# One set of four PSUM banks for units and down products, turned router products and a first gather of one expert pair in a two-layer decoder with a mixture of experts

## The chip, the cores and the metric

One core of a Trainium2 chip runs the whole program. The metric is device time in microseconds; a time is the median of several executions. TensorE (PE) multiplies matrices and writes into PSUM, which is divided here into eight banks of 512 float32 per partition; VectorE (DVE) and ScalarE (ACT) read the banks and write SBUF; GpSimd (POOL) computes a little and starts the indirect loads; the sync engine (SP) starts the loads of weights. Each engine works off its own instructions in program order and waits on semaphores for the others.

## What is computed

Two layers on 512 tokens of 1024 elements. Each layer has a mixer (attention and gated linear attention behind one projection) and then a mixture of 32 experts, four groups of eight: the router picks one group per token and two experts in it. The change lies in the second half.

```python
grp_prob = softmax(hf @ w_router_grp + b_router_grp)
grp_w, grp_idx = top_k(grp_prob, 1)
exp_logits = (hf @ w_router_exp + b_router_exp).reshape(-1, N_GROUPS, EXPERTS_PER_GROUP)
sel_logits = take_along_axis(exp_logits, grp_idx[:, :, None], axis=1)[:, 0]
top_logit, top_idx = top_k(sel_logits, 2)
top_w = softmax(top_logit) * grp_w
...
for g in range(N_GROUPS):
    a = einsum('nd,edf->nef', hf, w_gate[g])
    u = einsum('nd,edf->nef', hf, w_up[g])
    y = y + einsum('nef,efd->nd', silu(a) * u * comb[:, g, :, None], w_down[g])
```

Here `hf` is the normalised and modulated token, `comb` holds each token's weight for each expert (nought but for two), and `x = x + gate_f * y` ends the layer.

## The kernel before

Tokens stand in four tiles of 128 (`tt`), the 1024 elements in eight blocks of 128 (`k`). The kernel computes each expert on its own tokens only: 64 slots per expert, two experts (a pair) side by side in 128 rows, 16 pairs per layer. What would not fit in 64 slots goes through a loop at the end, which runs no iteration with these inputs.

**Router products.** `logits` (L860) runs while the mixer's output gets ready, for the first four `k`; `logits_of` (L874) does the last four `k` of one token tile. Both transpose `x` on PE into a bank of the tag `att` (three banks), copy it to SBUF (`xT`, by DVE and ACT in turns) and multiply it with the 36 columns of `wr`: tokens come out on the partitions, 36 logits each, all in one `misc` bank named `lg`. After that ACT writes the normalised tokens (`xn`, four operations at L923), and the POOL queue stores them to DRAM as `xg` (issued by the helper at L88). DVE makes `lo` out of `lg` (L937), one operation for each token tile.

**Selection** (L940 to L998, and L1207 on). DVE finds the group (`first_max`, L941), the two experts (`eid`, `ex`) and, with counting products on PE (`rk`), the slot of every token (`pos`, `slot`). `ohp` is a table of ones at the slots; `by_slot` (L1213) multiplies it with token numbers (`exn`) and gives a list of which token stands in which slot (`nv`), and `numbered` (L994) turns that into row numbers `idx`. `keep_warm` (L80) puts products whose result nobody reads into PE's queue. `fetch` (L1000) gathers 128 rows of `xg` by `idx`. The softmax weights of group and experts (`gs`, `gw`, `den`, `cw`) stand in the program behind the fetches.

**Expert loop.** `gather` (L1007) transposes fetched rows on PE into two banks of the tag `g` and evicts them with scale and shift to `gT`. Before the change it takes the rows of two pairs at a time, 256 columns, two `k` in a bank. `hidden` (L1035) makes the gate and up products (`gu`, one bank) and `hs`; `turn` (L1053) transposes `hs` and copies it to `hT`; `down` (L1062) makes two banks `d` of products and DVE scales them to `o`, which ACT and POOL split into `ohi` and `olo`; `places` (L1102) makes the table `oT` that brings slots back to tokens; `combine` (L1112) does one of eight units (a token tile and half of the columns): two products `y` into a bank, and DVE's `add` (L1092) onto `x`. `weights_by_slot` (L1248) comes once, behind the first pair's gate and up products.

In the program PE's order is: down products of pair i − 1, gate and up products of pair i, then the eight units of pair i − 1 with the transposes of rows for later pairs between them, and behind the sixth unit the transposes of `hs`:

```python
for u in range(4):
    for v in range(2):
        if i:
            combine(2 * u + v, *part)
    next(rest, None)
    if u == 2:
        hT = turn(hs)
```

PSUM in this half: `y` two banks (units, `keep_warm`, `slots`), `d` two, `g` two, `gu` one, `misc` one. A bank is taken again when everything that read it is done. `pm` and `tc.keep_in_program_order` pin the order of what they wrap; the rest may be moved by the scheduler between their dependences. The last two pairs are combined together by `combine_last` (L1120), whose units use banks of all tags.

SP's queue starts the weights: gate and up of an expert into one of five buffers `wgu`, down into one of four `wd`, four loads behind every `hidden`.

## Time and profile before

| | us |
|---|---|
| median of three runs | 1285.71 (1284.75 to 1287.04) |
| profiled execution, whole | 1283.96 |
| profiled execution, span of its instructions | 1282.1 |
| PE busy | 1172.3 (91%) |
| DVE busy | 797.0 (62%) |
| ACT busy | 462.7 (36%) |
| POOL busy | 307.0 (24%) |
| DMA, mean over the span | 244 GB/s |

The granted PE clock was 0.969 of full speed in the mean. A row of the page's groups reads: line, engine, operation, what is written and what is read, count; then busy time and mean ns of one; then the engine's idle time just ahead of these instructions and who ended most of it. PEld is PE's loading of stationary operands, which runs beside the products. A row of the order of time has the start, the busy time, and in brackets the idle time before it and its releaser. A product of float32 shows as two records in the trace. The lines that the argument rests on stand in the prediction.

### The profile page before, as it was taken

The numbers are of one execution on the slowest core, as the hardware profiler recorded it, in microseconds if no ns is written. First come the engines' busy times: TensorE is split into PE (matmuls) and PEld (weight loads), VectorE is DVE, ScalarE is ACT, GpSimd is POOL, SyncE is SP. The second block draws the span as 40 slices with busy tenths as digits, with TensorE's granted clock in tenths as the row PEclk, the third lists the DMA queues.
The fourth block names the chain that finished last, engine by engine and source line by source line (L and its number), as shares of the span: only waits on it lengthen the run. The fifth ranks groups of instructions, "written<-read, shape, count | busy, mean of one in ns | idle before, by whom it ended". The sixth has DMA issues, their size and how long they took to land. (4 is left out here: it accounts for less than half of the span.)

```text
span 1282.1 us, 16510 instructions
## 1 busy us (share of the span) xinstructions
PE 1172.3 (91%) x5935; PEld 739.7 (58%) x5935; DVE 797.0 (62%) x1484; ACT 462.7 (36%) x922; POOL 307.0 (24%) x330
## 2 busy tenths in 40 slices
PE   4989978977998999999988999899998899999996
PEld 2677746655885444444447877667787444444443
DVE  3488969796544555555546988877655355555553
ACT  3366635553251111111124775554535111111111
POOL 2122232244212222221103212434421222112110
PEclk9989989998979999999998999999998999999999
DMA  8454675751485999999805547763158699999961
GB/s 282 149 178 129 205 188 161 233 160 55 186 342 174 390 394 392 392 392 376 325 1 175 161 127 227 169 172 129 50 217 325 219 385 399 399 392 386 387 253 67
DMA packets 106285, 312.28 MB, mean 244 GB/s; under 512 B 13176, under 2 KB 50284, under 8 KB 81624
## 3 DMA queue, kind: packets, MB, share of 16 engines
q1 hardware_dynamic: 96920, 289.62, 62.6%
q0 software_dynamic: 9280, 21.57, 4.9%
q8 instruction: 48, 0.79, 0.3%
q14 instruction: 37, 0.30, 0.1%
HBM read 311.10 MB, written 8.43 MB: 249 GB/s over the span
## 5 line engine op out<-in xcount | busy, mean ns | idle before, releaser
L74 PE MATMUL proj<-whl,hh 128*128 128x512 f32 (+2 forms) x768 | 220.6, 370 | 7.4 <-ACT whl L95 6.2
L78 PE MATMUL gu<-wgu,gT 128*64 128x512 f32 x1024 | 225.8, 593 | 0.0
L1095 DVE TENSOR_TENSOR x<-y,x 128x512 f32<-128x512 f32 x240 | 153.9, 684 | 14.1 <-PE y L78 14.1
L78 PEld LDWEIGHTS gu<-wgu,gT 128*64 128x64 f32 x1024 | 73.5, 137 | 146.1 <-issue 146.1
L74 PEld LDWEIGHTS proj<-whl,hh 128*128 128x128 f32 x768 | 135.5, 191 | 36.1 <-issue 7.7
L1088 POOL TENSOR_TENSOR olo<-o,ohi 128x512 fp32r<-128x512 f32 x60 | 76.4, 1274 | 301.8 <-ACT ohi L1087 301.8
L96 POOL TENSOR_TENSOR whl<-raw,whl 128x512 fp32r<-128x512 f32 (+2 forms) x80 | 90.0, 1128 | 238.3 <-ACT whl L95 184.4
L1050 DVE TENSOR_TENSOR hs<-hs,gu 128x256 f32<-128x256 f32 x32 | 13.5, 421 | 204.4 <-ACT hs L1049 204.4
L74 PE MATMUL proj<-whl,hl 128*128 128x512 f32 (+2 forms) x384 | 139.0, 363 | 0.1
L255 DVE SCALAR_TENSOR_TENSOR row<-wada,ct,row 128x512 f32<-128x512 f32 x140 | 119.9, 856 | 16.8 <-DMA wada<-in_w_ada_dram 15.6
L78 PE MATMUL y<-ohi,oT 128*128 128x512 f32 x240 | 116.1, 484 | 6.9 <-DVE x L1095 6.9
L78 PE MATMUL d<-wd,hT 128*64 128x512 f32 x512 | 116.9, 598 | 1.4 <-ACT hT L1059 1.4
L1028 ACT ACTIVATE gT<-g,mod 128x256 f32<-128x256 f32 x64 | 35.9, 565 | 177.3 <-DVE gT L1030 177.3
L78 PE MATMUL y<-olo,oT 128*128 128x512 f32 x240 | 94.6, 394 | 0.0
L95 ACT ACTIVATE whl<-raw 128x512 fp32r<-128x512 f32 (+2 forms) x128 | 66.2, 524 | 68.3 <-PE proj L74 36.6
L78 PEld LDWEIGHTS y<-ohi,oT 128*128 128x128 f32 x240 | 44.8, 186 | 74.8 <-DVE x L1095 45.4
L74 PEld LDWEIGHTS proj<-whl,hl 128*128 128x128 f32 x384 | 72.6, 189 | 13.4 <-issue 3.0
L1049 ACT ACTIVATE hs<-gu 128x256 f32<-128x256 f32 x32 | 12.3, 384 | 169.9 <-PE gu L78 169.9
L78 PEld LDWEIGHTS d<-wd,hT 128*64 128x64 f32 x512 | 33.9, 136 | 62.2 <-issue 59.9
L1082 DVE SCALAR_TENSOR_TENSOR o<-d,cws,gate_f 128x512 f32<-128x512 f32 x64 | 47.7, 748 | 34.9 <-PE d L78 34.9
L1087 ACT ACTIVATE ohi<-o 128x512 fp32r<-128x512 f32 x60 | 37.8, 629 | 78.9 <-DVE o L1082 78.8
L1003 POOL DMA_INDIRECT rows<-xg,idx x32 | 32.8, 1025 | 126.0 <-PE g L1022 108.9
(339 smaller groups left out, 2041.6 us busy)
## 6 DMA issues: line engine op xcount, KB each, us to landing
wgu<-in_w_gate_dram SPq DMA_DIRECT2D x64, 1024.0 KB, 7.7
wgu<-in_w_up_dram SPq DMA_DIRECT2D x64, 1024.0 KB, 10.3
wd<-in_w_down_dram SPq DMA_DIRECT2D x64, 1024.0 KB, 8.8
wada<-in_w_ada_dram SPq DMA_DIRECT2D x96, 512.0 KB, 4.3
raw<-in_w_in_dram SPq DMA_DIRECT2D x80, 256.0 KB, 3.6
raw<-in_w_out_dram SPq DMA_DIRECT2D x16, 512.0 KB, 3.7
raw<-in_w_in_dram SPq DMA_DIRECT2D x32, 128.0 KB, 2.9
xg<-xn POOLq DMA_DIRECT2D x8, 512.0 KB, 2.9
```

The lines of the kernel that those rows point to most:

```text
L74: T.matmul(o, a, b, start=start, stop=stop, skip_group_check=True)
L78: tc.keep_in_program_order(T.matmul(o, a, b, start=start, stop=stop, skip_group_check=True))
L95: A.activation(hi, src, AF.Copy)
L96: eng.tensor_tensor(lo, src, hi.bitcast(F), op=OP.subtract)
L255: V.scalar_tensor_tensor(row, ws[k], ct1[:, k:k + 1], row, op0=OP.mult, op1=OP.add)
L1003: G.indirect_dma_start(r, None, xg[:, :], bass.IndirectOffsetOnAxis(ap=idx, axis=0), bounds_check=S - 1, oob_is_err=False)
L1028: A.activation(o, src, AF.Identity, scale=m, bias=b)
L1050: V.tensor_tensor(hs[r], hs[r], gu[r, 256:512], op=OP.mult)
L1082: V.scalar_tensor_tensor(o, pd, cws[:, i:i + 1], gate, op0=OP.mult, op1=OP.mult)
L1087: A.activation(hi, o, AF.Copy)
L1088: (G if last is None else V).tensor_tensor(lo, o, hi.bitcast(F), op=OP.subtract)
L1095: V.tensor_tensor(xc, ps, xc, op=OP.add)
```

## The change

It has five parts.

1. `logits` and `logits_of`: `wr` is now the stationary operand and `xT` the moving one, so that 36 logits come out on the partitions and tokens along the row. Even `k` add up on partitions 0 to 35, odd `k` on 64 to 99 of the same bank (`lgT`). For each token tile GpSimd clears a tile, DVE copies the one part and ACT the other into it, and one product with the constant `two_parts` adds both and turns them round into `lg`, which now takes one of the three `att` banks. `lo` is made in two operations over all tiles.
2. The list: token numbers start at 1 − 65536, so that `numbered` is one operation for the whole list; `ohp` is one table of 64 columns per entry, and `by_slot` makes two products of 64 by 16 where one of 128 by 32 was; the last `keep_warm` has 20 products, not 14.
3. The softmax weights are issued behind the list.
4. The first gather takes the rows of the first pair alone (128 columns, four `k` in a bank); the second pair's is put behind the first pair's gate and up products.
5. `y`, `d`, `warm` and `slots` share one tag `dy` of four banks.

The diff, cut to its core:

```diff
@@ keep_warm, down, combine, add_rows, weights_by_slot
-        ps = bank("warm", "y", 2)
+        ps = bank("warm", "dy", 4)
...
-                pd = bank("d", "d", 2)
+                pd = bank("d", "dy", 4)
...
-            ps = bank("y", "y", 2)
+            ps = bank("y", "dy", 4)
...
-                ps = bank("slots", "y", 2)
+                ps = bank("slots", "dy", 4)
@@ constants
+    two_parts = const.tile([P, 36], F, name="two_parts")
+    V.tensor_tensor(two_parts, ident[:, 0:36], ident[:, 64:100], op=OP.add)
...
-    G.iota(tok_i, pattern=[[P, NT]], base=1, channel_multiplier=1)
+    G.iota(tok_i, pattern=[[P, NT]], base=1 - 65536, channel_multiplier=1)
@@ logits
-            for tt in range(NT):
-                mm(lg[:, tt], t[:, P * tt:P * tt + P], wr[:, k], tt == 0 and k == 0, k == KT - 1)
+            o = 64 * (k % 2)
+            mm(lg[0][o:o + 36], wr[:, k], t, k < 2, False)
@@ logits_of
+        c = slice(P * tt, P * tt + P)
         for k in range(4, KT):
-            mm(lg[:, tt], t[:, P * (k - 4):P * (k - 3)], wr[:, k], False, k == KT - 1)
+            o = 64 * (k % 2)
+            mm(lg[0][o:o + 36, c], wr[:, k], t[:, P * (k - 4):P * (k - 3)], False, k >= KT - 2)
+        t = s2([P, P], name="lgT")
+        G.memset(t, 0.0)
+        if lg[1] is None:
+            lg[1] = att("lg")[:, 0:NT * 36].rearrange("p (t e) -> p t e", t=NT)
+        for i, copy in enumerate((V.tensor_copy, A.copy)):
+            r = slice(64 * i, 64 * i + 36)
+            copy(t[r], lg[0][r, c])
+        mm(lg[1][:, tt], t, two_parts, tt == 0, True)
@@ moe
-        for tt in range(NT):
-            V.scalar_tensor_tensor(lo[:, tt], lg[:, tt], rs[:, tt:tt + 1], lc, op0=OP.mult, op1=OP.add)
+        V.tensor_tensor(lo, lg, rs[:, :, None].to_broadcast([P, NT, 36]), op=OP.mult)
+        V.tensor_tensor(lo, lo, lc[:, None, :].to_broadcast([P, NT, 36]), op=OP.add)
@@ numbered
-            none = tiny.tile(list(idx.shape), F, name="none")
-            V.tensor_scalar(none, ps, 0.0, 65536.0, op0=OP.is_equal, op1=OP.mult)
-            V.scalar_tensor_tensor(idx, ps, -1.0, none, op0=OP.add, op1=OP.add)
+            return V.tensor_scalar(idx, ps, 65535.0, None, op0=OP.add)
@@ gather
-                for k2 in range(KT // 2):
+                nk = 512 // n
+                for k0 in range(0, KT, nk):
...
-                    for k in (2 * k2, 2 * k2 + 1):
+                    for k in range(k0, k0 + nk):
@@ by_slot and the list
-            lst = misc(name, [P, NE])
+            lst = misc(name, [P, NE // 2])
             for i in range(NT * 2):
-                pm(lst, ohp[i // NT][:, i % NT].rearrange("p a s -> p (a s)"), values[:, i], i == 0, i == NT * 2 - 1)
+                for a in range(2):
+                    pm(lst[64 * a:64 * a + 64], ohp[:, i], values[:, i, a::2], i == 0, i == NT * 2 - 1)
...
-        nv = by_slot(exn, "nv")
-        for a in range(2):
-            numbered(nv[64 * a:64 * a + 64, :, a], idx[64 * a:64 * a + 64])
-        keep_warm(lo.rearrange("p t e -> p (t e)"), 14)
+        listed = numbered(by_slot(exn, "nv"), idx)
+        keep_warm(lo.rearrange("p t e -> p (t e)"), 20)
...
+        with tc.issue_after(listed.ins):
...
@@ first pairs
-        gT, rest = gather(fetched[0:2])
+        gT, rest = gather(fetched[0:1])
         for _ in rest:
             pass
+        gT1, second = gather(fetched[1:2])
...
             if i == 0:
+                for _ in second:
+                    pass
                 weights_by_slot()
```

What is left out: the first two pairs read their tokens from column 0 of `gT` and `gT1`, `combine_last` and the loop for overflow name `dy` where they named `y` and `d`, and the lines of the softmax weights are indented under `issue_after`.

Three places show how instructions move. In these rows, each is one engine's instruction with its output, its inputs and its size, an `x` with a count where it repeats, and in brackets the engines or DMA queues whose semaphores it waits for. The first is PE's queue at the end of one burst in the middle of layer 0's loop: `y` are the units' products, `g` transposed rows, `d` the down products. Before:

```order
L78 MATMUL y<-ohi,oT 128x512 [waits DVE_49]
L78 MATMUL y<-olo,oT 128x512
L78 MATMUL y<-ohi,oT 128x512 [waits DVE_49]
L78 MATMUL y<-olo,oT 128x512
L1022 MATMUL g<-ident,rows 128x128 x2
L78 MATMUL d<-wd,hT 64x512 [waits DMAHW0_49,Activation_49]
L78 MATMUL d<-wd,hT 64x512 [waits DMAHW1_49]
L78 MATMUL d<-wd,hT 64x512 x2
L78 MATMUL d<-wd,hT 64x512 [waits PE_49]
L78 MATMUL d<-wd,hT 64x512 x3
```

After:

```order
L78 MATMUL y<-ohi,oT 128x512 [waits DVE_49]
L78 MATMUL y<-olo,oT 128x512
L78 MATMUL y<-ohi,oT 128x512 [waits DVE_49]
L78 MATMUL y<-olo,oT 128x512
L1035 MATMUL g<-ident,rows 128x128 x2
L78 MATMUL d<-wd,hT 64x512 [waits DMAHW0_49,DVE_49,Activation_49]
L78 MATMUL d<-wd,hT 64x512 [waits DMAHW1_49]
L78 MATMUL d<-wd,hT 64x512 x2
L78 MATMUL d<-wd,hT 64x512 [waits DVE_49]
L78 MATMUL d<-wd,hT 64x512 x3
```

The order is the same; the first `d` and the fifth now wait for DVE as well, where the fifth waited for PE before.

The second is PE's queue at the end of layer 0's router products: `xT` are the transposes of `x`, `lg` and `lgT` the products with `wr`, `warm` the products of `keep_warm`. Before:

```order
L74 MATMUL lg<-wr,xT 128x36 [waits DVE_49]
L74 MATMUL lg<-wr,xT 128x36 x3
L879 MATMUL xT<-ident,x 128x128 x3
L74 MATMUL lg<-wr,xT 128x36 [waits Activation_49]
L74 MATMUL lg<-wr,xT 128x36 x3
L879 MATMUL xT<-ident,x 128x128 [waits PE_49]
L879 MATMUL xT<-ident,x 128x128 x3
L74 MATMUL lg<-wr,xT 128x36 [waits DVE_49]
L74 MATMUL lg<-wr,xT 128x36 x3
L74 MATMUL lg<-wr,xT 128x36 [waits Activation_49]
L74 MATMUL lg<-wr,xT 128x36 x3
L78 MATMUL warm<-lo,ident 128x144 [waits DVE_49]
```

After (the lines of the code have moved by four):

```order
L883 MATMUL xT<-ident,x 128x128 [waits PE_49]
L883 MATMUL xT<-ident,x 128x128 x3
L74 MATMUL lgT<-xT,wr 36x128 [waits Activation_49]
L74 MATMUL lgT<-xT,wr 36x128 x3
L883 MATMUL xT<-ident,x 128x128 [waits PE_49]
L883 MATMUL xT<-ident,x 128x128 x3
L74 MATMUL lg<-two_parts,lgT 128x36 [waits Activation_49]
L74 MATMUL lgT<-xT,wr 36x128 x4
L74 MATMUL lg<-two_parts,lgT 128x36 [waits Activation_49]
L74 MATMUL lgT<-xT,wr 36x128 x4
L74 MATMUL lg<-two_parts,lgT 128x36 [waits Activation_49]
L78 MATMUL warm<-lo,ident 128x144 [waits DVE_49]
```

Each token tile's four products are now followed by one that waits for ACT; the last tile's transposes stand between the second tile's products and that one.

The third is DVE's queue in the selection of layer 0, from the second expert's index `bix` to the sum of the two experts' ones `both`. Before:

```order
L947 TENSOR_REDUCE bix<-boh 128x4 [waits DVE_49]
L1228 TENSOR_REDUCE gs<-gd 128x4 [waits Activation_49]
L1237 TENSOR_SCALAR den<-e_3606 128x4 [waits Activation_49]
L966 SCALAR_TENSOR_TENSOR eid<-gix,bix 128x4 [waits DVE_49]
L1230 RECIPROCAL gw<-gs 128x4 [waits DVE_49]
L1238 RECIPROCAL den<-den 128x4 [waits DVE_49]
L967 TENSOR_TENSOR ex<-iota_96,eid 128x4x32 [waits DVE_49]
L1239 TENSOR_TENSOR cw<-den,gw 128x4 [waits DVE_49]
L1240 TENSOR_TENSOR e_3606<-e_3606,den 128x4
L969 TENSOR_TENSOR both<-ex 128x128 [waits DVE_49]
```

After:

```order
L961 TENSOR_REDUCE bix<-boh 128x4 [waits DVE_49]
L980 SCALAR_TENSOR_TENSOR eid<-gix,bix 128x4 [waits DVE_49]
L981 TENSOR_TENSOR ex<-iota_98,eid 128x4x32 [waits DVE_49]
L983 TENSOR_TENSOR both<-ex 128x128 [waits DVE_49]
L985 TENSOR_TENSOR exn<-ex,tok 128x256
```

The six operations on the softmax weights and their waits for ACT (`gs`, `den`, `gw`, `cw`, and the one on `e`) have left this place; they stand behind the list's `idx` now.

More of the change, by code (lines that the diff above doesn't have):

```diff
@@ L863, in logits @@
         if lg is None:
-            lg = route[l][2] = misc("lg", [P, NT, 36])
+            lg = route[l][2] = [misc("lgT"), None]
         for k in ks:
@@ L917, in moe @@
         load_weights(9)
-        wr, lc, lg = route.pop(l)
+        wr, lc, (_, lg) = route.pop(l)
         rs = inv_rms(ss)
@@ L1020, in make @@
                         for j, r in enumerate(fetched):
-                            at = n * (k % 2) + P * j
+                            at = n * (k - k0) + P * j
                             tc.keep_in_program_order(T.transpose(ps[:, at:at + P], r[:, P * k:P * k + P], ident))
-                    for k in (2 * k2, 2 * k2 + 1):
-                        src = ps[:, n * (k % 2):n * (k % 2) + n]
+                    for k in range(k0, k0 + nk):
+                        src = ps[:, n * (k - k0):n * (k - k0) + n]
                         m, b = mod[l][:, 4, k:k + 1], mod[l][:, 5, k:k + 1]
@@ L1122, in combine_last @@
             order = [units[u] for u in (0, 2, 4, 6, 1, 3, 5, 7)]
-            tags = [("y", 2), ("y", 2), ("g", 2), ("g", 2), ("gu", 1), ("misc", 1), ("d", 2), ("d", 2)]
+            tags = [("dy", 4), ("dy", 4), ("g", 2), ("g", 2), ("gu", 1), ("misc", 1), ("dy", 4), ("dy", 4)]
             ps = {}
@@ L1161, in add_rows @@
                 for q in range(2):
-                    ps = bank("y", "y", 2)
+                    ps = bank("y", "dy", 4)
                     mm(ps, wT[0:n, P * tt:P * tt + P], o[q][0:n], True, True)
@@ L1202, in overflow_lists @@
             V.memset(xslot, 0.0)
-        ohp = [ohl([P, NT, 2, CAP], name="ohp") for _ in range(2)]
-        for h in range(2):
-            places_h = pos.rearrange("p t k -> p (t k)")[:, NT * h:NT * h + NT, None, None]
-            tc.keep_in_program_order(V.tensor_tensor(ohp[h], iota[:, None, None, 0:CAP].to_broadcast([P, NT, 2, CAP]),
-                                                     places_h.to_broadcast([P, NT, 2, CAP]), op=OP.is_equal))
+        ohp = ohl([P, NT * 2, CAP], name="ohp")
@@ L1211, in by_slot @@
+        tc.keep_in_program_order(V.tensor_tensor(ohp, iota[:, None, 0:CAP].to_broadcast([P, NT * 2, CAP]),
+                                                 pos.rearrange("p t k -> p (t k)")[:, :, None].to_broadcast([P, NT * 2, CAP]),
+                                                 op=OP.is_equal))
         def by_slot(values, name):
-            lst = misc(name, [P, NE])
+            lst = misc(name, [P, NE // 2])
             for i in range(NT * 2):
-                pm(lst, ohp[i // NT][:, i % NT].rearrange("p a s -> p (a s)"), values[:, i], i == 0, i == NT * 2 - 1)
@@ L1236, in moe @@
-        den = t3(1, "den")
-        V.tensor_scalar(den, e2, 1.0, None, op0=OP.add)
-        V.reciprocal(den, den)
-        V.tensor_tensor(cw[:, :, 0:1], den, gw, op=OP.mult)
-        V.tensor_tensor(e2, e2, den, op=OP.mult)
-        V.tensor_tensor(cw[:, :, 1:2], e2, gw, op=OP.mult)
-        dump(f"cw{l}", cw)
-        exw = tmp.rearrange("p t k e -> p (t k) e")
-        V.tensor_tensor(exw, ex.rearrange("p t k e -> p (t k) e"), cw.rearrange("p t k -> p (t k)")[:, :, None].to_broadcast([P, NT * 2, NE]), op=OP.mult)
+        with tc.issue_after(listed.ins):
+            gs = t3(1, "gs")
+            A.activation(ge, ge, AF.Exp)
+            V.reduce_sum(gs, ge, axis=AX.X)
+            gw = t3(1, "gw")
+            V.reciprocal(gw, gs)
+            cw = t3(2, "cw")
+            e2 = t3(1, "e2")
+            V.tensor_tensor(e2, m2, m1, op=OP.subtract)
+            A.activation(e2, e2, AF.Exp)
+            tc.keep_in_program_order(A.preload_act_table_set("silu_and_others"))
+            den = t3(1, "den")
+            V.tensor_scalar(den, e2, 1.0, None, op0=OP.add)
+            V.reciprocal(den, den)
+            V.tensor_tensor(cw[:, :, 0:1], den, gw, op=OP.mult)
+            V.tensor_tensor(e2, e2, den, op=OP.mult)
+            V.tensor_tensor(cw[:, :, 1:2], e2, gw, op=OP.mult)
+            dump(f"cw{l}", cw)
+            exw = tmp.rearrange("p t k e -> p (t k) e")
+            V.tensor_tensor(exw, ex.rearrange("p t k e -> p (t k) e"), cw.rearrange("p t k -> p (t k)")[:, :, None].to_broadcast([P, NT * 2, NE]), op=OP.mult)
@@ L1276, in moe @@
                 part = places(i - 1), down(hT, [loaded.pop((1, e)) for e in (2 * i - 2, 2 * i - 1)], i - 1)
-            *_, hs = hidden(now, P * (i % 2), [loaded.pop((0, e)) for e in (2 * i, 2 * i + 1)])
+            *_, hs = hidden(gT1 if i == 1 else now, 0 if i < 2 else P * (i % 2), [loaded.pop((0, e)) for e in (2 * i, 2 * i + 1)])
             load_weights(4)
```

17 lines of the change are left out of this document (3 added, 14 removed).

## The prediction

> **What bounds the kernel.** I read the groups of instructions on the page first, for where TensorE (PE) stands still, then the order of time in one iteration of the expert loop, then the busy time by windows for the DMA engines, and last the order of time between router and first expert. All times are of the profiled execution. Of a timeline row the first number is the start, the second the busy time.
>
> ```profile
> L1095 DVE TENSOR_TENSOR x<-y,x 128x512 f32<-128x512 f32 x240 | 153.9, 684 | 14.1 <-PE y L78 14.1
> L78 PE MATMUL y<-ohi,oT 128*128 128x512 f32 x240 | 116.1, 484 | 6.9 <-DVE x L1095 6.9
> L78 PEld LDWEIGHTS y<-ohi,oT 128*128 128x128 f32 x240 | 44.8, 186 | 74.8 <-DVE x L1095 45.4
> ...
> 523.31 0.50 PE L78 MATMUL y<-ohi,oT 128*128 128x512 f32 x1
> ...
> 524.95 0.50 PE L78 MATMUL y<-ohi,oT 128*128 128x512 f32 x1 [0.22 <-DVE x L1095]
> ...
> 527.63 0.38 PE L1022 MATMUL g<-ident,rows 128*128 128x128 f32 x2
> 527.85 0.40 PE L1057 MATMUL hsT<-ident,hs 128*128 128x128 f32 x2
> 528.11 0.50 PE L78 MATMUL y<-ohi,oT 128*128 128x512 f32 x1
> ...
> 529.28 0.38 PE L1022 MATMUL g<-ident,rows 128*128 128x128 f32 x2
> 529.59 1.08 PE L78 MATMUL d<-wd,hT 128*64 128x512 f32 x4
> ```
>
> Between an expert pair's gate/up products (`gu`) and the next down products (`d`), PE works off a burst: eight units of two products (`y`), eight transposes of gathered rows (`g`) and two of `hs`. It lasts 529.59 − 523.31 = **6.28 us**. PE's weight loads for `y` wait 45.4 us in all for VectorE's (DVE's) `add`, which frees one of two banks; on PE itself only 6.9 us appear, because the late weight load spreads the products instead of leaving a gap. What the products take when banks are there stands at the end of the loop, where `combine_last` has eight of them:
>
> ```profile
> 657.41 0.40 PE L78 MATMUL y<-ohi,oT 128*128 128x512 f32 x1
> ...
> 659.27 0.39 PE L1057 MATMUL hsT<-ident,hs 128*128 128x128 f32 x2
> ...
> 412.45 1.51 PE L78 MATMUL d<-wd,hT 128*64 128x512 f32 x6 [0.24 <-ACT hT L1059]
> ...
> 640.46 0.50 PE L78 MATMUL y<-ohi,oT 128*128 128x512 f32 x1
> 646.38 1.08 PE L78 MATMUL d<-wd,hT 128*64 128x512 f32 x4
> ...
> 445.91:462.65 16.74, 16.53 (x76) 7.22 (x75) 8.86 (x16) 3.15 (x6) 2.55 (x2) 1.00 0.99 398
> ```
>
> Eight products in 659.27 − 657.41 = 1.86 us, 0.233 each. In the window (one iteration; its last three numbers are granted clock, DMA share and GB/s) PE is busy 16.53 of 16.74 us: the loop goes at PE's pace. From 412.45 to 646.38 lie (233.93 / 16.74 =) 14 iterations, so 14 bursts; the last has no `g` and lasts 646.38 − 640.46 = 5.92 us.
>
> **The change, part 1: one set of four banks.** A unit now waits for the bank of four units back, not two. PE alone needs 16 × 0.233 = 3.72 us for the products, 4 × 0.22 for `g` (527.63 to 527.85), 0.26 for `hsT` (to 528.11) and 0.09 more ahead of `d` (0.31 against 0.22): 4.95 us. The price is that `d` takes its two banks from the same set, and so waits for the adds of units four and five, counted from nought, instead of finding its own banks free. DVE's rows tell whether that is late:
>
> ```profile
> 524.21 1.28 DVE L1095 TENSOR_TENSOR x<-y,x 128x512 f32<-128x512 f32 x2
> 525.72 1.29 DVE L1095 TENSOR_TENSOR x<-y,x 128x512 f32<-128x512 f32 x2 [0.23 <-PE y L78]
> 526.93 0.54 DVE L1030 TENSOR_SCALAR gT<-g,mod 128x256 f32<-128x256 f32 x1
> 527.38 1.28 DVE L1095 TENSOR_TENSOR x<-y,x 128x512 f32<-128x512 f32 x2
> ```
>
> The first add starts 0.90 us behind the burst's start, one takes 0.64, and a `gT` holds the adds up 0.45 (526.93 to 527.38). The add of unit four ends at 0.90 + 5 × 0.64 + 0.45 = 4.55, that of unit five at 5.19, and the second bank of `d` is wanted four products (one `d` takes about 0.27: 1.08 for four) after the first. So DVE stays 0.4 us ahead of PE. Behind a waiting `d` stand all of PE's next `gu`, so a late add would cost PE its whole delay. I take 5.15, with 0.2 for this meeting: 1.13 us less per burst; the ends are 1.33 (4.95) and 0.22 (only the gap seen on PE goes). The last burst: 3.72 + 0.26 + 0.09 = 4.07, with the adds at 4.1; I take 4.2, 1.7 less. Per layer 13 × 1.13 + 1.7 = 16.4, both layers **−32.8**; with 1.33 and 1.85 it is −38.3, with 0.22 throughout −6.
>
> That cover has a second condition, the weights.
>
> ```profile
> 412.00:416.00 4.00, 3.76 (x20) 1.26 (x20) 3.93 (x11) 1.40 (x3) 0.00 (x0) 1.00 1.01 426
> ...
> 630.00:634.00 4.00, 4.00 (x21) 1.43 (x22) 3.70 (x7) 1.19 (x2) 0.38 (x1) 1.00 0.26 107
> ```
>
> The DMA share is 0.99 at 398 GB/s. At 16.74 − 1.13 = 15.61 us the same bytes want 427; the first window shows 426. It is just enough. The last weights are there when DMA falls idle, by 634, while the last `gu` follows the `d` of 646.38, so the loads have more than 12 us in hand, which is nearly the 14.7 that thirteen bursts give back. I cost it at nothing; without this cover, below.
>
> **Part 2: first rows alone.** The way from the index list to the first `gu`:
>
> ```profile
> 389.93 1.42 POOL L1003 DMA_INDIRECT rows<-xg,idx  x1 [5.86 <-DVE idx L998]
> ...
> 394.69 0.33 PE L1022 MATMUL g<-ident,rows 128*128 128x128 f32 x1 [2.35 <-DMA rows<-xg,idx]
> 396.48 1.47 PE L1022 MATMUL g<-ident,rows 128*128 128x128 f32 x7 [1.46 <-DMA rows<-xg,idx]
> ...
> 400.24 1.08 PE L78 MATMUL gu<-wgu,gT 128*64 128x512 f32 x4
> ...
> 994.12 1.09 POOL L1003 DMA_INDIRECT rows<-xg,idx  x1 [5.72 <-DVE idx L998]
> ...
> 997.61 0.33 PE L1022 MATMUL g<-ident,rows 128*128 128x128 f32 x1 [1.61 <-DMA rows<-xg,idx]
> ...
> 1003.37 1.12 PE L78 MATMUL gu<-wgu,gT 128*64 128x512 f32 x2
> ```
>
> Fetch to `gu` is 10.31 us in layer 0 and 9.25 in layer 1. The second pair's rows (the wait ended at 396.48) and eight of 16 transposes leave this way. What stays is the fetch's landing (3.49 in layer 1; 4.76 in layer 0, whose fetch instruction ran 1.42 instead of 1.09, so I take 3.9) and eight transposes, 8 × 0.11 (from 0.22 for two) and 0.2 for the first eviction: 1.1. That is 5.0 and 4.6, so −5.3 and −4.65. Given back behind `gu`: eight transposes, 0.9, and weight lists of twice as many, half as wide products, 0.3: **−4.1 and −3.45**.
>
> **Part 3: router, selection, and a new last wait.** The list no longer waits for ScalarE's (ACT's) exponentials nor, where PE's clock holds, for the slow `nv`:
>
> ```profile
> 377.65 0.74 DVE L937 SCALAR_TENSOR_TENSOR lo<-lg,rs,lc 128x36 f32<-128x36 f32 x4 [5.09 <-PE lg L74]
> ...
> 978.95 0.74 DVE L937 SCALAR_TENSOR_TENSOR lo<-lg,rs,lc 128x36 f32<-128x36 f32 x4 [2.47 <-PE lg L74]
> ...
> 986.04 0.17 DVE L1228 TENSOR_REDUCE gs<-gd 128x4 f32<-128x16 f32 x1 [2.27 <-ACT gd L1227]
> ...
> 992.52 0.37 DVE L997 TENSOR_SCALAR none<-nv 64x16 f32<-64x16 f32 x2 [1.49 <-PE nv L78]
> ...
> 987.46 3.23 PE L78 MATMUL warm<-lo,ident 128*128 128x144 f32 x12
> ...
> 374.38 0.59 ACT L881 COPY xT<-xT 128x512 f32<-128x512 f32 x1 [4.38 <-PE xT L879]
> 374.86 8.39 ACT L923 ACTIVATE xn<-x,rs 128x1024 f32<-128x1024 f32 x4
> ...
> 987.66 0.42 DVE L983 TENSOR_TENSOR tmp<-ex,rk 128x256 f32<-128x256 f32 x1 [0.20 <-PE rk L78]
> ...
> xg<-xn POOLq DMA_DIRECT2D x8, 512.0 KB, 2.9
> ...
> 367.15 1.76 PE L74 MATMUL lg<-wr,xT 128*128 128x36 f32 x8
> ...
> 973.13 1.08 PE L74 MATMUL lg<-wr,xT 128*128 128x36 f32 x8
> ```
>
> From `lo` to the fetch layer 1 takes 994.12 − 978.95 = 15.17 us; without the two waits and the `none` it is 15.17 − 2.27 − 1.49 − 0.37 = 11.0, and one of two `ohp` goes besides, while twice as many products for the list bring about as much. But the fetch also needs `xg`, and `xn` on ACT now queues behind the last of the new copies of logits, about 0.6 us ahead of `lo` (before: 2.8 ahead in layer 0). Four `xn` take 8.39, the last store's issue 0.3, its landing 2.9 by the page's median: −0.6 + 8.4 + 0.3 + 2.9, so `lo` + 11.0, and the fetch 0.2 later. **The store ends with the list or behind it**, and a faster list would bring nothing more. Behind that fetch on GpSimd's queue stand the other three fetches, and PE's transposes wait for them.
>
> `lo` itself: the products stay much as they are (36 stationary columns and 512 or 128 moving instead of 128 and 36), but each token tile now makes a round: its second half of products (eight records, 1.08 together in layer 1, now in two column groups side by side: about 0.5), 0.2 until they are seen (the wait of `tmp` for `rk`), a DVE and then an ACT copy of 128 columns (0.185 for 36 columns by `lo`, 0.59 for 512 by `xT`: about 0.27 each), and the product with `two_parts`, about 0.35 with its way out: 1.6 us. PE does its queue in order, and behind the waiting `two_parts` product stand the next tiles' products; so the four rounds are in series, 6.4 us, and I count 1.5 us for transposes that no copy hides. From the start of the second halves: 973.13 + 6.4 + 1.5 + 0.2 = 981.2 in layer 1 (+2.3), and with 0.5 for the lower clock 367.15 + 6.4 + 1.5 + 0.5 = 375.6 in layer 0 (−2.0). Ends: +6 if the rounds take 0.9 us more each, −3 if the copies are covered. GpSimd's four memsets lie where its queue waits for `xn` anyway.
>
> Fetch in layer 0: 375.6 + 11.2 = 386.8 (−3.1). Layer 1: its stores share DMA with other loads; I take a landing of 4.0: 981.2 + 12.3 = 993.5 (−0.6). Front: −3.1 − 4.1 − 0.6 − 3.45 = **−11.2**; with the ends of `lo`, −14 and −3.
>
> **Sum.** 1283.96 − 32.8 − 11.2 = 1239.96 for the profiled execution. The median of the runs, 1285.71, is 1.75 above it: **1241.7**, said as 1241.5.
>
> **Rivals.**
> 1. DMA is at its end (0.13). For it: a share of 0.99 in the loop. If 398 GB/s were all, the loads would fall 1.13 us behind per iteration, 14.7 in thirteen, and use up their 12 in hand in the last three; with rows that come late (a second wait inside the burst), 4 us per layer come back: 1249.5.
> 2. The front gives nothing (0.14): the round of four tiles costs its +6, `xg` lands at 5 us, and the fetch comes later by what the first rows save. 1241.5 + 11 = 1252.5. For it: three engines hand over in series. Against: layer 0's long stretch has room.
> 3. Half clock (0.10): twelve warming products took 3.23 us in layer 1, 0.27 each, at the lower clock; 40 of them take 10.8 and end some 5 us behind the rows' arrival: 1241.5 + 10 = 1251.5. For it: eight `lg` took 1.76 in layer 0 and 1.08 in layer 1, with PE busy in both. [...]
> 4. Slower (0.04): `d` waits for the burst's last adds and not for the fourth and fifth. The adds end at 0.90 + 8 × 0.64 + 0.45 = 6.5, with the second `gT` 7.0 and what `d` needs of DVE behind it 7.5: +1.2 per burst, 28 bursts, +33.6, less 11 of the front: 1308. It decides when the add of four units back ends later than 4.95 us behind the burst's start; DVE's rows put it at 4.55.
> 5. The change does not do what it says (0.05): `y` waits move one bank on and half of them stay, as DVE's 6.5 us per burst exceed PE's: −16 in the loop, 1258.
>
> My forecast has 0.52, and within it I would not be off by more than 8 us. The range reaches up to cases 1, 2, 3 and 5, and down to the favourable ends, 38.3 in the loop and 14 in front: 1285.7 − 52.3 = 1233.4: **1233 to 1261**. Faster by over 0.2% (2.6 us, about what a measurement can tell from no change): 0.52 + 0.13 + 0.14 + 0.10 + 0.05 = 0.94; slower: 0.04, case 4; within 0.2%: the 0.02 that is left, for several cases at once.
>
> **What would show it.** The burst from first `y` to `d` at about 5.15 and the iteration at 15.6; PE's weight loads waiting for `add` under 10 us in all, and a short wait of `d` for DVE; DMA share unchanged at a higher rate. `lo` near 375.6 and, with layer 0's 20 or so us less, 960; the fetch released by `xg` and not by `idx`; `gu` 5 us behind it. The prediction is wrong if `d` waits over 0.5 us for DVE, if `gu` waits for DMA, or if `lo` to the first `gu` is no shorter than before (22.6 and 24.4 us).

## The result and the profile after

The changed kernel takes 1244.96 us (median of 4 runs, 1230.81 to 1246.43) where the kernel before takes 1286.38 (1284.75 to 1287.26): a ratio of 0.9663, 95% interval 0.9624 to 0.9702. In a second series on another occasion it was 1236.86 (6 runs) against 1284.36, 0.9643 (0.9605 to 0.9681). Forecast were 1241.5 and a range of 1233 to 1261. Single executions of either kernel lie some 15 us apart: over all series the kernel before has 43 executions from 1276.48 to 1291.78 with a mean of 1284.9, the changed one ten from 1230.81 to 1246.43 with a mean of 1239.2. One execution of a kernel further below (`old_router`, 1250.41) was in a slower state, over 1.5% above the fastest of that kernel, and is left out of its mean and ratio. So below, a stretch is compared with the same stretch of several traces, and means stand beside medians.

The rows of the after page's groups that answer to the first three of the prediction (after the bar: busy time and mean ns; then the engine's idle time before and who ended it), then one burst of the loop on PE and on DVE, one iteration by windows, and the end of the loads in layer 0 with the last `gu` of that layer:

```profile
L1108 DVE TENSOR_TENSOR x<-y,x 128x512 f32<-128x512 f32 x240 | 148.3, 679 | 0.9 <-PE y L78 0.9
...
L78 PE MATMUL y<-ohi,oT 128*128 128x512 f32 x240 | 104.8, 437 | 0.0
...
L78 PEld LDWEIGHTS y<-ohi,oT 128*128 128x128 f32 x240 | 45.4, 189 | 31.9 <-issue 26.0
```

```profile
523.65 0.51 PE L78 MATMUL y<-ohi,oT 128*128 128x512 f32 x1
...
527.90 0.39 PE L78 MATMUL y<-ohi,oT 128*128 128x512 f32 x1
...
528.36 0.38 PE L1035 MATMUL g<-ident,rows 128*128 128x128 f32 x2
528.67 1.51 PE L78 MATMUL d<-wd,hT 128*64 128x512 f32 x6
...
524.55 2.48 DVE L1108 TENSOR_TENSOR x<-y,x 128x512 f32<-128x512 f32 x4
526.94 0.53 DVE L1043 TENSOR_SCALAR gT<-g,mod 128x256 f32<-128x256 f32 x1
527.39 2.47 DVE L1108 TENSOR_TENSOR x<-y,x 128x512 f32<-128x512 f32 x4
...
451.31:466.78 15.47, 15.47 (x76) 7.33 (x75) 8.57 (x16) 3.05 (x6) 4.56 (x4) 1.00 1.01 417
...
616.00:620.00 4.00, 4.00 (x20) 2.88 (x17) 2.95 (x6) 0.57 (x2) 0.00 (x0) 1.00 0.07 27
...
624.13 2.32 PE L78 MATMUL gu<-wgu,gT 128*64 128x512 f32 x10
```

PE no longer waits for an add of the loop, neither in the open (6.9 us before, none now) nor in the weight loads of `y` (45.4 us of waits for DVE before; of the 31.9 left, 26.0 are PE's own issue). The burst lasts 528.67 − 523.65 = 5.02 us, was 6.28. DVE does four adds in a row without a break, 0.62 each, where it had pairs with gaps between them. In the window PE is busy all of the 15.47 us, and the DMA share is 1.01 at 417 GB/s: the share was 0.99 at 398 before, so a share near 1 was no sign of a full DMA. The loads end by about 616, 8 us ahead of the last `gu`.

The way from router to first expert, in layer 0:

```profile
375.01 0.31 DVE L950 TENSOR_TENSOR lo<-lg,rs 128x144 f32<-128x144 f32 x1 [0.80 <-PE lg L74]
...
383.14 0.53 POOL L88 DMA_DIRECT2D xg<-xn  x1 [1.52 <-ACT gd L1239]
386.90 1.11 POOL L1015 DMA_INDIRECT rows<-xg,idx  x1 [3.23 <-DVE tmp L1256]
...
384.23 0.17 DVE L1010 TENSOR_SCALAR idx<-nv 128x16 int32<-128x16 f32 x1 [0.49 <-PE nv L78]
...
391.18 1.09 PE L1035 MATMUL g<-ident,rows 128*128 128x128 f32 x8 [1.89 <-DMA rows<-xg,idx]
392.34 7.16 PE L78 MATMUL gu<-wgu,gT 128*64 128x512 f32 x32
```

and in layer 1:

```profile
964.69 0.31 DVE L950 TENSOR_TENSOR lo<-lg,rs 128x144 f32<-128x144 f32 x1 [0.80 <-PE lg L74]
...
973.91 0.17 DVE L1010 TENSOR_SCALAR idx<-nv 128x16 int32<-128x16 f32 x1 [0.49 <-PE nv L78]
...
974.50 0.54 POOL L88 DMA_DIRECT2D xg<-xn  x1 [3.18 <-ACT e L1246]
978.39 1.09 POOL L1015 DMA_INDIRECT rows<-xg,idx  x1 [3.34 <-DMA xg<-xn]
...
983.10 8.85 PE L78 MATMUL gu<-wgu,gT 128*64 128x512 f32 x32
```

The list `idx` is done 2.5 and 4.3 us before the fetch begins; what the fetch waits for is the last store of `xg`, named in the row of layer 1. In layer 0 the row names DVE, whose `tmp` had nothing to do with the fetch. But there too the store issued last, at 383.14, takes 2.9 us to land, and the fetch begins 0.9 us behind the landing, as in layer 1 (2.9 and 1.0).

The span cut into its stretches, in the first trace of each, beside the prediction:

| stretch (us) | before | after | difference | predicted |
|---|---|---|---|---|
| up to layer 0's first router transposes | 361.32 | 361.17 | −0.15 | 0 |
| from there to its first down products | 51.13 | 43.73 | −7.40 | −7.2 |
| first to last down products, layer 0 | 247.67 | 229.47 | −18.20 | −16.4 |
| mixer: from there to layer 1's first router transposes | 307.51 | 316.48 | +8.97 | 0 |
| from there to its first down products | 48.44 | 46.50 | −1.94 | −4.05 |
| first to last down products, layer 1 | 247.61 | 229.46 | −18.15 | −16.4 |
| tail | 18.42 | 16.69 | −1.73 | 0 |
| span | 1282.1 | 1243.5 | −38.6 | −44 |

### The profile page after: what moved, and what is told of

Same layout as the page of the kernel before. It is cut to its first block, busy times and chain, and to the rows that moved or that the text cites. A ratio compares the mean times of both kernels' runs of the same rounds, so it can differ in the third digit from the quotient of the medians.

```text
span 1243.5 us, 16659 instructions
## 1 busy us (share of the span) xinstructions
PE 1139.8 (92%) x5991; PEld 733.5 (59%) x5991; DVE 799.8 (64%) x1487; ACT 465.5 (37%) x938; POOL 307.5 (25%) x338
## 5 line engine op out<-in xcount | busy, mean ns | idle before, releaser
L74 PE MATMUL proj<-whl,hh 128*128 128x512 f32 (+2 forms) x768 | 225.1, 376 | 9.5 <-ACT whl L95 7.2
L78 PEld LDWEIGHTS gu<-wgu,gT 128*64 128x64 f32 x1024 | 76.1, 138 | 144.8 <-issue 143.4
L74 PEld LDWEIGHTS proj<-whl,hh 128*128 128x128 f32 x768 | 138.3, 195 | 39.3 <-ACT whl L95 8.4
L1108 DVE TENSOR_TENSOR x<-y,x 128x512 f32<-128x512 f32 x240 | 148.3, 679 | 0.9 <-PE y L78 0.9
L78 PE MATMUL y<-ohi,oT 128*128 128x512 f32 x240 | 104.8, 437 | 0.0
L1062 ACT ACTIVATE hs<-gu 128x256 f32<-128x256 f32 x32 | 12.3, 385 | 170.1 <-PE gu L78 170.1
L78 PEld LDWEIGHTS y<-ohi,oT 128*128 128x128 f32 x240 | 45.4, 189 | 31.9 <-issue 26.0
L1041 ACT ACTIVATE gT<-g,mod 128x256 f32<-128x256 f32 (+1 forms) x72 | 38.9, 544 | 65.8 <-DVE gT L1043 65.7
L1095 DVE SCALAR_TENSOR_TENSOR o<-d,cws,gate_f 128x512 f32<-128x512 f32 x64 | 47.5, 745 | 21.7 <-PE d L78 21.7
```

The lines of the kernel that those rows point to most:

```text
L74: T.matmul(o, a, b, start=start, stop=stop, skip_group_check=True)
L78: tc.keep_in_program_order(T.matmul(o, a, b, start=start, stop=stop, skip_group_check=True))
L1041: A.activation(o, src, AF.Identity, scale=m, bias=b)
L1095: V.scalar_tensor_tensor(o, pd, cws[:, i:i + 1], gate, op0=OP.mult, op1=OP.mult)
L1108: V.tensor_tensor(xc, ps, xc, op=OP.add)
```

## The experiments

Twelve runs followed. The theory after the comparison: loop and front give what the table says, and the 9 us of layer 1's mixer, in which not one instruction was changed or moved, are no effect of the change. The rival: the change does it to the mixer.

### Once more, and the two halves by themselves

`after_again` is the changed kernel, `before_again` the kernel before.

> The changed kernel once more. Both theories: bursts of 5.02 us, 229.5 us per layer from the first to the last down products, the first down products of layer 0 about 43.7 us behind the first transposes of its router products (361.17 to 404.90 in the first trace). Theory 1 (the 8.9 us that the mixer of layer 1 lost, with not one instruction changed in it, are the luck of one execution): from the last down products of layer 0 to the first router transposes of layer 1 something between 305 and 318 us, another value than 316.5, and times of single executions that spread from 1231 to 1247. Theory 2 (the change does it to the mixer, by the phase in which it starts it): 316.5 again, and executions at 1245, with 1231 a rare one.

> The kernel before once more, for a second trace of the mixer of layer 1: theory 1 (luck of an execution) lets it differ from 307.6 us by several us; theory 2 has 307.6 again, within 0.5.

`banks_alone` is the kernel before with the one set of banks, `front_alone` the changed kernel without it:

```diff
-                pd = bank("d", "d", 2)
+                pd = bank("d", "dy", 4)
...
-            ps = bank("y", "y", 2)
+            ps = bank("y", "dy", 4)
```

> The kernel before with the one set of four banks alone. If the parts add up: 229.5 us per layer from the first to the last down products (247.7 before), -36.4 in all, the router to first expert as before (layer 0: 51.1 us from the first router transposes to the first down products), so 1286 - 36 = 1250 if the mixer of layer 1 takes its 307.6, 1259 if it takes 316.5. If the loads' lead is what carries the loop (rival: DMA at its end), the last iterations get longer than 15.47.

> The changed kernel with the banks as before (two for units, two for down products). If the parts add up: iterations of 16.73 us, layer 0's first down products 7.5 us earlier, layer 1's 1.8 earlier by its own stretch, no other term: 1286 - 9.4 = 1276.6; the mixer of layer 1 at 307.6 if the loop's phase was what disturbed it, at 316.5 (1285.5 in all) if it is the front that does it.

| kernel | executions, mean | ratio (95%) | router to d, layer 0 | layer 1 | loop | mixer 0 | mixer 1 | tail |
|---|---|---|---|---|---|---|---|---|
| before | 43, 1284.9 | | 51.13 | 48.44 | 247.67 | 361.32 | 307.51 | 18.42 |
| before_again | 1, 1276.1 | | 50.05 | 48.06 | 247.69 | 353.40 | 308.98 | 18.37 |
| after | 4, 1241.8 | 0.9663 (0.9624 to 0.9702) | 43.73 | 46.50 | 229.47 | 361.17 | 316.48 | 16.69 |
| after_again | 6, 1237.5 | 0.9643 (0.9605 to 0.9681) | 44.08 | 44.84 | 229.46 | 353.78 | 313.28 | 16.71 |
| banks_alone | 6, 1245.7 | 0.9701 (0.9653 to 0.9749) | 50.06 | 49.64 | 229.21 | 358.71 | 308.16 | 18.42 |
| front_alone | 11, 1274.7 | 0.9924 (0.9895 to 0.9953) | 45.56 | 44.81 | 247.66 | 357.19 | 315.03 | 16.69 |

The loop's gain belongs to the banks alone and is the same to 0.3 us wherever they are; the front's belongs to the front. The means add up within their spread: 1245.7 − 1284.9 = −39.2 (expected −36) and 1274.7 − 1284.9 = −10.2 (expected −9.4) make −49.4, the whole change has 1239.2 − 1284.9 = −45.7, with standard deviations of 3 to 7 us of single executions. Mixer 0 differs by 8 us between two executions of one kernel (361.32 and 353.40). Mixer 1 was not 316.5 again, but it did not fall to 308 either; more on it at the end of this section.

### What the banks are worth

```diff
-                pd = bank("d", "dy", 4)
+                pd = bank("d", "dy", 2)
...
-            ps = bank("y", "dy", 4)
+            ps = bank("y", "dy", 2)
```

and the same with 3, for all users of the set.

> The changed kernel with the shared set cut to two banks for units, down products, warming and slots (the units of the last two pairs that need a place take two banks of their own). Theory (the sharing itself costs nothing, it is the number of banks that pays): iterations of 16.7 to 16.9 us, as with two for units and two for down products. Rival (down products wait for the burst's last adds when they share): 17.3 to 17.9.

> The changed kernel with a shared set of three banks. By the timing of the adds (first add 0.90 us behind the burst's start, 0.62 each, 0.45 for a gT) the add of three units back ends before the product that needs its bank for all units, and the add of unit five ends at 4.98, where the first down product is wanted at 5.02: iterations of 15.47 to 15.6, so the fourth bank is worth nothing. Rival (every bank helps): about halfway, 16.1.

Iterations of 16.79 us with two banks, 15.82 with three, 15.47 with four; 16.73 with two and two apart. Sharing costs 0.06 us per iteration, even where two banks must do for both. The theory on three banks missed: 15.82, not 15.47 to 15.6. In a burst of `dy3`, the row of the first `y` and the rows of PE's weight loads and of DVE tell why:

```profile
537.18 0.50 PE L78 MATMUL y<-ohi,oT 128*128 128x512 f32 x1
...
538.82 0.19 PEld L78 LDWEIGHTS y<-ohi,oT 128*128 128x128 f32 x1 [0.19 <-DVE x L1108]
...
540.01 0.19 PEld L78 LDWEIGHTS y<-ohi,oT 128*128 128x128 f32 x1 [0.20 <-DVE x L1108]
...
541.66 0.19 PEld L78 LDWEIGHTS y<-ohi,oT 128*128 128x128 f32 x1 [0.43 <-DVE x L1108]
...
540.48 0.54 DVE L1043 TENSOR_SCALAR gT<-g,mod 128x256 f32<-128x256 f32 x1
540.93 2.48 DVE L1108 TENSOR_TENSOR x<-y,x 128x512 f32<-128x512 f32 x4
```

The last unit waits 0.43 us for the add of three units back, the first one behind the `gT`; it starts at 540.93 and takes 0.62, so it ends 4.37 us behind the burst's start. I had that add about right (0.90 + 5 × 0.62 + 0.45 = 4.45); what was wrong is that it would end before the last unit wants its bank. With four banks that unit starts at 4.25 (527.90 − 523.65 above). Two weight loads before it wait 0.2 us each, but their units start no more than 0.01 us later than with four banks. So the fourth bank is worth 0.35 us per iteration, some 10 us in all, mostly because a `gT` stands between the adds.

### The first gather

```diff
-        gT, rest = gather(fetched[0:1])
+        gT, rest = gather(fetched[0:2])
```

and no gather of its own for the second pair.

> The changed kernel with the first gather over two pairs as before. By the prediction's step: gate and up products 5.0 to 5.3 us later behind the fetch (10 us instead of 4.7 to 5.7), 1.2 of it given back behind them, so the first down products 4 us later per layer, +8 in all, mean 1247. Rival (rows and transposes were covered by the warming products or by the fetch's wait): under 2 us per layer.

Gate and up products 9.51 and 9.75 us behind the fetch, and the first down products 46.61 and 49.90 us behind the first router transposes: 2.7 later than the mean of the two traces of the changed kernel in layer 0 and 4.2 in layer 1. Mean of four executions 1244.5 (expected 1247), 5.3 above the changed kernel's ten; ratio 0.9702 (0.9656 to 0.9749), whose interval overlaps the changed kernel's, so the times alone do not show the loss. By the stretches the step holds; in layer 0 it was 1.3 too large. The trace of layer 0 has the wait again that the change took away:

```profile
381.62 0.33 PE L1035 MATMUL g<-ident,rows 128*128 128x128 f32 x1 [1.81 <-DMA rows<-xg,idx]
383.19 1.50 PE L1035 MATMUL g<-ident,rows 128*128 128x128 f32 x7 [1.24 <-DMA rows<-xg,idx]
385.06 1.97 PE L1035 MATMUL g<-ident,rows 128*128 128x128 f32 x8 [0.38 <-ACT gT L1041]
386.96 7.09 PE L78 MATMUL gu<-wgu,gT 128*64 128x512 f32 x32
```

### The router products and the list

`old_router` has the router products of before:

```diff
-            o = 64 * (k % 2)
-            mm(lg[0][o:o + 36], wr[:, k], t, k < 2, False)
+            for tt in range(NT):
+                mm(lg[:, tt], t[:, P * tt:P * tt + P], wr[:, k], tt == 0 and k == 0, k == KT - 1)
```

> The changed kernel with the router products as before (no copies of logits, no product with two_parts), all else changed. Theory (the turned router products cost time and hold the stores up): the first lo 11.3 us behind the first router transposes (13.8 to 14.1 changed), the list's idx at 20.5 (23.1 to 23.4), the last store issued at 18.6 in layer 0 and 20.2 in layer 1, the fetch at 22 in layer 0 and 24 in layer 1 (25.8 and 27.5), the first down products about 40.5 and 42 us behind the first transposes (44.0 and 45.5 in the mean): 7 us less than the changed kernel, mean of executions 1232. Rival (the long lo of the first trace of before, 16.3 us at half clock, is the rule): lo at 16 in layer 0, and no gain or a loss of 2 us.

`lo` comes 11.31 us behind the first transposes in both layers, not 13.84 to 14.08; the last store is issued at 18.56 and 20.23, the fetch goes at 23.25 and 24.75, the first down products at 41.50 and 43.48. The turned products cost 2.5 us at `lo`, and 2.4 and 2.2 at the end of the stretch. Not quite 5 us in all, where 7 were expected, are too few for the times to show (mean of five executions 1234.8 against 1239.2, ratio 0.9617, 0.9561 to 0.9673). Four other traces with the old products (`before_again`, `before_third`, `banks_alone`, `constant`) have `lo` of layer 0 at 11.3 too; the 16.3 of the first trace of before, from which I started, was one execution's low clock. The windows from the first transposes to `lo`, in that trace and in `before_again`, show it (the granted clock is the third number from the end):

```profile
361.32:377.65 16.33, 16.16 (x97) 15.77 (x95) 4.09 (x11) 6.40 (x12) 0.31 (x1) 0.65 0.86 346
```

```profile
353.40:364.72 11.32, 11.12 (x97) 10.50 (x95) 4.09 (x10) 4.94 (x11) 0.00 (x0) 1.00 0.96 384
```

`old_list` has the list and the softmax weights of before, with the turned router products.

```diff
-        listed = numbered(by_slot(exn, "nv"), idx)
-        keep_warm(lo.rearrange("p t e -> p (t e)"), 20)
+        nv = by_slot(exn, "nv")
+        for a in range(2):
+            numbered(nv[64 * a:64 * a + 64, :, a], idx[64 * a:64 * a + 64])
+        keep_warm(lo.rearrange("p t e -> p (t e)"), 14)
...
-        with tc.issue_after(listed.ins):
```

> The changed kernel with list and softmax weights as before (two ohp, nv of 128 by 32, none and idx in two steps, 14 warming products, exponentials ahead of the list). Theory (the faster list brings little, as the store ends last): idx 2 to 4 us later (25.5 to 27.5 behind the first router transposes), the fetch 0.5 to 1 behind it, the first down products 0 to 1.5 later per layer. For the mixer of layer 1: 313 to 316.5 if the list has nothing to do with its 5 us, 307 to 309 if it has.

That missed: `idx` comes at 29.85 and 28.17, 6.6 and 4.9 us later than in the mean of the changed kernel's two traces, and the fetch goes with it. The first down products are at 49.52 and 46.70. Two rows of layer 0 show it:

```profile
373.96 0.17 DVE L1243 TENSOR_REDUCE gs<-gd 128x4 f32<-128x16 f32 x1 [3.02 <-ACT gd L1242]
...
382.67 1.15 POOL L1017 DMA_INDIRECT rows<-xg,idx  x1 [8.03 <-DVE idx L1012]
```

ACT works off `xn` behind the copies of logits, and the exponentials behind `xn`; DVE, whose order has `gs` ahead of the list, waits 3.02 us for them. But the kernel before had most of that wait too: 2.2 to 2.3 us in every front except layer 0 of its first trace (0.90, where `lo` itself was late). So the turned products add only 0.8 us to it, and the miss is mainly that the changed list saves more than I had counted: from the start of `lo` to the end of `idx` layer 1 takes 14.7 us here, 14.0 to 14.6 in five traces with the whole old front, and 9.4 to 9.6 in five with the changed one. Which part of the list brings how much was not tested. In the end the list is worth 5.6 us in layer 0 and 1.0 in layer 1, where the store ends later; about 1.7 of the 5.6 may be that execution's own, as layer 0 took 16.4 us from `lo` to `idx` with a granted clock of 0.50 from 366 to 383 us, and layer 1 14.7.

`xn_split` tests the wait for the store: the old router products, and two of the four `xn` on DVE, with `lo` pinned behind them.

```diff
+            xk = xt[tt // 2][:, tt % 2].rearrange("t (p k) -> t k p", k=KT)
+            if tt % 2:
+                tc.keep_in_program_order(V.tensor_scalar(xn, xk, rs[:, tt:tt + 1], None, op0=OP.mult))
+            else:
+                A.activation(xn, xk, AF.Copy, scale=rs[:, tt:tt + 1])
```

> The changed kernel with the old router products (the constant two_parts gone too) and two of the four xn on DVE, ahead of lo, instead of all four on ACT. Theory (the fetch waits for the last store, not for the list): the last store issued near 14.5 us behind the first router transposes (18.6 and 20.2 with all xn on ACT), the fetch 0.4 behind idx, at 21 to 22 (23.25 and 24.75), the first down products 2 us earlier in layer 0 and 3 in layer 1 (39.5 and 40.5), 5 us less than with the old router alone. Rival (the list decides, or DVE's xn delays lo by as much): the fetch stays at 23 to 25.

The last store goes at 15.0 and 16.55, and the fetch now follows the list: 22.30 and 22.61, against an `idx` at 21.85 and 21.62. The wait for the store is gone, which shows that it was one. DVE's two `xn` took 2.22 us and put `lo` off by 1.1, so that layer 0 gained nothing on `old_router` (41.41), where 2 us were expected; layer 1 gained 3.0 us (40.52), 1.1 of them because the first `gu` took 7.16 us and not 8.27. The mean of six executions is 1235.8, ratio 0.9615 (0.9584 to 0.9646): by its stretches 2.5 us in layer 0 and 5.1 in layer 1 better than the mean of the changed kernel's two traces, by its time not clear of it, as the intervals overlap.

### The mixer of layer 1

`constant` is the kernel before with one constant more, that nothing reads; `before_third` the kernel before.

```diff
+    two_parts = const.tile([P, 36], F, name="two_parts")
+    V.tensor_tensor(two_parts, ident[:, 0:36], ident[:, 64:100], op=OP.add)
```

> The kernel before with nothing but the constant two_parts added (144 bytes per partition, so that what is allocated behind it may lie elsewhere in SBUF). For the mixer of layer 1: 313 to 316.5 if places in SBUF make its 5 us, 307 to 309 if they do not. All else as in the kernel before.

> The kernel before a third time, for the mixer of layer 1 alone: two traces of it have 307.5 and 309.0 us from the last down products of layer 0 to the first router transposes of layer 1, the kernel with a constant more had 317.8, the changed one 316.5 and 313.3. If an execution's luck decides, this one may lie anywhere from 305 to 318; if places in SBUF do, it lies at 307 to 309.

The last down products of layer 0 and the first router transposes of layer 1, in `constant` and then in `before_third`:

```profile
652.66 3.65 PE L78 MATMUL d<-wd,hT 128*64 128x512 f32 x16 [0.46 <-ACT hT L1061]
...
970.47 1.47 PE L870 MATMUL xT<-ident,x 128*128 128x128 f32 x12
```

```profile
657.23 2.36 PE L78 MATMUL d<-wd,hT 128*64 128x512 f32 x9 [0.46 <-ACT hT L1059]
...
966.32 1.47 PE L868 MATMUL xT<-ident,x 128*128 128x128 f32 x12
```

317.8 and 309.1 us. The four traces in which nothing is laid out otherwise than before (three of the kernel before and `banks_alone`) have 307.5 to 309.1; the ten others, among them `constant`, have 313.2 to 317.8. So, if `constant` is no accident, it is neither the router products nor the list nor the gather: one unused constant does as much. That places in SBUF do it is the obvious reading, but only argued: `constant` ran once, and the times do not bear it out. If layer 1's mixer cost 6 us in every execution of `front_alone`, its own terms (about −4.5 and −3.8 in the fronts, −1.7 in the tail) would leave −4 in the mean, and −10.2 was measured over eleven executions. What decides it stays open. In the first trace after, DVE waits longer for the adaLN weights there (the rows of before and after, in the mixer of layer 1 alone):

```profile
L255 DVE SCALAR_TENSOR_TENSOR row<-wada,ct,row 128x512 f32<-128x512 f32 x56 | 44.6, 797 | 5.6 <-DMA wada<-in_w_ada_dram 5.1
```

```profile
L258 DVE SCALAR_TENSOR_TENSOR row<-wada,ct,row 128x512 f32<-128x512 f32 x56 | 47.1, 841 | 9.1 <-DMA wada<-in_w_ada_dram 8.6
```

That wait does not go with the length of the stretch, though: `before_again` has 8.4 us of it in 309.0, `constant` 6.3 in 317.8. The granted clock goes with it roughly: 0.97 to 0.98 in the four short traces, 0.95 to 0.97 in the ten long ones. Whether that is cause or effect is not shown.

## Why the prediction was right, point by point

- **The burst.** Right in mechanism, small in size: 5.02 us, not 5.15, so −36.4 in both loops and not −32.8. The mis-sized term is the 0.2 us that I added for `d` meeting DVE's adds. The adds of units four and five end about 4.4 and 5.0 us behind the burst's start (the second four begin at 527.39, 0.62 each); the first of them is wanted at 5.02 and the second more than a microsecond later, so DVE is ahead of PE and `d` waits for nobody. The profile does name DVE ahead of one weight load of `d` per burst, but that gap is no longer than the gap before the next load, which waits for nothing:

```profile
530.01 0.14 PEld L78 LDWEIGHTS d<-wd,hT 128*64 128x64 f32 x2 [0.29 <-DVE x L1108]
530.44 0.14 PEld L78 LDWEIGHTS d<-wd,hT 128*64 128x64 f32 x2 [0.29 <-issue]
```

- **Rival 4**, `d` behind the burst's last adds, fell with the same rows, and by `dy2`: even with two banks for all, sharing costs 0.06 us.
- **Rival 1**, DMA at its end: thirteen iterations per layer take 15.47 us, at 417 GB/s, and no `gu` waits for DMA. The loads kept a lead, but a smaller one: they ended some 18 us ahead of the last `gu` before (DMA share 0.05 from 632 to 634, last `gu` at 649.87) and end 8 us ahead now.
- **The fetch.** `lo` at 375.01 for 375.6, the fetch at 386.90 for 386.8 in layer 0. That the fetch is so close is luck: it comes 11.9 us behind `lo`, not 11.2, because it begins 0.9 and not 0.2 us behind the store's landing, and `lo` was 0.6 early. That the store and not the list would end last is confirmed by both layers and by `xn_split`. In layer 1 the fetch comes 13.7 us behind `lo`, not 12.3: the last store was issued 9.8 us behind `lo`, where layer 0 has 8.1. Its landing takes 2.9 us as in layer 0, not the 4.0 of the sum; so the mis-sized term is the issue. The last `xn` ends equally late in both layers (21.7 us behind the first transposes), so ACT's work on it is not what delays the store. All traces but the first of before, whose layer 0 is the one with the low clock, have such a difference between the layers (18.6 and 20.2 with the old router products); its cause was not looked for further.
- **`lo`.** The turned products cost what I worked out, 13.84 us against 11.3 in layer 1 (+2.5 for +2.3). The −2.0 in layer 0 was worked out from the one trace of before with the low clock; against the other traces it is +2.5 there too. The half of the time that I took off the second half of products, for two column groups side by side, was my estimate, and no run shows that they run so: the eight records took 0.63 us for the 0.5, and from the second round on the rounds followed each other in 1.75 us for the 1.6.
- **Fetch to first expert.** 5.44 and 4.71 us for 5.0 and 4.6. What is given back behind it was predicted with +1.2 and measured with +0.35 in layer 0, because the weight list got cheaper, not dearer (in layer 1 of the first trace after it is +1.55, with the slow `gu` below). Rows of before, then of after:

```profile
407.26 1.97 PE L78 MATMUL lst<-tmp,ohp 128*128 128x32 f32 x16
```

```profile
400.45 1.11 PE L78 MATMUL lst<-tmp,ohp 128*64 128x16 f32 x32
```

  Twice as many products of half the columns took 1.11 us instead of 1.97. The same made `nv` cheaper: 1.11 us for 32 records, 1.94 for 16 before, in layer 0 (granted clock 1.00 in both).
- **Rivals 2 and 5.** The front gave 9.3 us in the first traces, not nothing, where 11.2 were forecast. That layer 0 came out as forecast (−7.4 for −7.2) is luck in part, as both are counted from the slowest of the old traces. Over the five traces that have the old front in each layer, the stretch from router to first down products takes 50.1 and 48.7 us, over the five with the changed front 44.9 and 45.4: 5.3 and 3.3 us less, 8.6 in all. And no wait of PE for an add is left in the loop, not half of them.
- **Clock (rival 3).** The 40 warming records took 5.17 us after, at a granted clock of 1.00, and did not reach into the rows' arrival. But in the first trace after, PE stood 2.98 us before the first transposes of layer 1, and the gate and up products behind them took 8.85 us instead of 7.16, with a granted clock of 0.81. In `after_again` PE stood 2.60 us there, and the products took 7.16. How long PE stands does not decide it alone: layer 0 of `after_again` and of `dy2` have nearly the same gap.

```profile
384.14 1.09 PE L1035 MATMUL g<-ident,rows 128*128 128x128 f32 x8 [1.92 <-DMA rows<-xg,idx]
385.30 7.16 PE L78 MATMUL gu<-wgu,gT 128*64 128x512 f32 x32
```

```profile
391.02 1.09 PE L1035 MATMUL g<-ident,rows 128*128 128x128 f32 x8 [1.94 <-DMA rows<-xg,idx]
392.18 8.85 PE L78 MATMUL gu<-wgu,gT 128*64 128x512 f32 x32
```

  In the ten fronts of the five traces with the changed front, five have 7.15 to 7.16 us for these products and five 8.20 to 8.85. What decides it is not shown: nearly the same gap costs one execution 1.7 us and another nothing, and layer 0's `lo` came at 16.3 in one trace of before and at 11.3 in two others. The row of eight `lg` in 1.76 us, which stands for this rival, lies in the stretch with the granted clock of 0.65; the same products and transposes ran at 1.00 in `before_again`, so this work alone does not make the low clock.
- **What I had not counted.** Layer 1's mixer (+9.0) and the tail (−1.7) in the first trace. There the loop gave 3.6 us more than forecast and the front 1.9 less, so that without the mixer the span would have come out shorter than forecast. In the means of all executions it looks otherwise: −36.4 in the loops, −8.6 in the fronts and −1.7 in the tail make −46.7, and −45.7 was measured, so nothing like 9 us is left for the mixer. That the total of −44.0 came so close is in part luck: the front was forecast 2.6 us too large, the loop 3.6 too small.

## What to carry to other kernels

Products that fill banks and an engine that empties them need as many banks as the emptying engine is ever behind, counted at its worst place: here the one eviction that stands between two groups of adds made most of the 0.35 us per iteration that the fourth bank is worth. Two users of PSUM that take turns in a fixed order can share one set at almost no cost (0.06 us per iteration here), and each then has the other's banks while it works.

Where several things must be ready for one step, shortening the one that ends last hands the step to the next: here the list was cut, and the store of the normalised tokens took its place. The copies that the change added ahead of it on ACT's queue made it later still, 22.0 us behind the first transposes in layer 0 against 18.6, though it ended last without them too (`old_router`).

A stretch of one trace is one execution. Here identical instructions took 353 or 361 us in one place and 307 or 309 in another; terms of a few microseconds should be read from two traces before they are summed.
